# Hybrid encoder layer on one core: order of the down projection's splits, one head norm's precedence, the place of small products, and the end of the last tile but one

## The chip, the cores and the metric

The kernel runs on one core of a Trainium2 chip. The metric is the device time of one execution in microseconds (us). The core has a matrix engine (TensorE, PE), a vector engine (VectorE, DVE), a scalar engine (ScalarE, ACT), a general engine (GpSimd, POOL) and a sync engine (SyncE, SP) that here only issues DMAs; ScalarE and GpSimd issue some DMAs too. Each engine works through its own list of instructions in order; semaphores tie the lists together.

## The reference

One layer on an input x of 1024 rows of 1024 float32 numbers:

```python
h = rmsnorm(x, norm_mix_pre)
y = mixer(h, w_in, ...)            # short conv and gated linear attention, then @ w_out
x = x + rmsnorm(y, norm_mix_post)
h = rmsnorm(x, norm_ffn_pre)
y = conv_mlp(h, w_up, conv_ffn, w_down)
x = x + rmsnorm(y, norm_ffn_post)
```

The mixer projects h with w_in, runs a gated 3-tap convolution over 512 channels, and gated linear attention (GLA) forwards and backwards in chunks of 64 rows for 4 heads (key width 64, value width 128). Each head's output o is normalised over its 128 channels, `o * rsqrt(mean(o*o) + eps) * gla_head_norm`, and gated with silu. The feed-forward part (FFN) is `(silu(conv3(h W_up)_gate) * conv3(h W_up)_val) @ W_down` with an inner width of 2816.

## The kernel before

**Precision.** Each float32 operand of a large product is split into a high part in a reduced format and a low rest: `split` (L690) makes the high part as a cast on ScalarE (L691) and the low part as a subtraction on VectorE (L692). Each product takes three passes (high with high, high with low, low with high).

**Stages**, by their place in the trace: first norm and value projection 0 to 66 us, gates 66 to 111, GLA and convolution 111 to 325, output projection 325 to 440, FFN up in 22 columns 440 to 841, FFN down 841 to 1055, the last norm and the stores to 1063. A tile framework sets the order of each engine's list: it issues instructions by the program's order and by precedence, and buffers of a pool are handed on as they come free.

**GLA.** `feature_chunk` (L230) computes 128 columns of a projection, in 8 parts of 6 matmuls of 512 columns. After each part it takes one entry off a list `between` and issues it. `gla_head` (L478) appends three entries (L590): the eight products `kv` for the first half of the chunks, the eight for the second, and the 32 score products (sc). They need `koT`, a copy by ScalarE (L524). After each kv, ScalarE copies it into the states S (L565, L569), and VectorE runs the recurrence over them (L574, L578). A head's output `po` is then squared by ScalarE into `on`, and its norm follows (L614 to L616): a reduction on VectorE, the reciprocal square root in `rstd_of` (one-column steps: L175 and L177 on ScalarE, L176 and L181 to L184 on VectorE), and the product `on`. TensorE then transposes `on` (L622, into pot).

**FFN down.** A Strassen-like scheme replaces 8 block products by 7, numbered m. `big_product` (L1117) runs m = 2, 1, 3, 6, 5, 7, each over q = 0 to 10 with 12 matmuls of 512 columns. `operands(m, q)` (L1080) prepares one q: a raw tile from a small pool is filled by SyncE with a block of the activations (L1087) and one of the weights or of their sums (L1090 or its neighbour), and then split. Below, d2_4 stands for m = 2, q = 4; the profile cuts such names to d_4, d_4r (raw), d_4h and d_4l. For q = 10 of m = 1 and 2 the activation is still in SBUF. While this starts, the last FFN column is still worked on: its convolution (L965 to L967), its silu (L1045), its gate (L1048) and the sums that the scheme needs (L1060 to L1064), which ScalarE's queue stores (L1057, L1065, L1066). GpSimd computes sums of weight blocks (L128 to L131) and loads and stores their tiles.

**The end.** The seventh product (m = 4) is done by rows, output tile by output tile. For tiles 4 to 7 ScalarE squares the parts (L1203), VectorE multiplies by the gain (L1207) and adds parts (L1202), `rstd_of` follows, and `finish` (L1171) computes yg times the row's factor plus x2, the residual, in one VectorE instruction (L1174), and stores it. The last tile (t = 7) is worked in parts of 256 columns and finished in two halves.

Of the kernel before, what the change touches and what calls it, by code (L numbers as in the profile page):

```python
# [8 lines left out]
F32 = mybir.dt.float32  # L9
F32R = mybir.dt.float32r  # L10
I32 = mybir.dt.int32
AF = mybir.ActivationFunctionType
# [4 lines left out]
P = 128  # L17
# [3 lines left out]
NT = L // P  # L21
HALF = 512
HEADS = 4
DK = 64
DV = 128
# [4 lines left out]
NFC = FF // P  # L30
# [11 lines left out]
def kernel(  # L42
# [20 lines left out]
    nc = tc.nc  # L63
    x = x[0]
    out = out[0]
# [16 lines left out]
    def ps_tile(name):  # L82
        return psp.tile([P, 1024], F32, tag="ps", name=name)

    def act_tile(name):
        return actp.tile([P, KT, HALF], F32R, tag="act", name=name)
# [77 lines left out]
    def keep(ins):  # L164

        return tc.keep_in_program_order(ins) if pinned[0] else ins

    def rstd_of(ss, width, rest=None):

        n = ss.shape[1]  # L170
        v = small.tile([P, n], F32, tag=f"rv{n}", name="rv")
        a = small.tile([P, n], F32, tag=f"rs{n}", name="rs")
        t = small.tile([P, n], F32, tag=f"rt{n}", name="rt")
        bias = eps[:, 0:1] if rest is None else rest
        keep(nc.scalar.activation(a, ss, AF.Ln, bias=bias, scale=1.0 / width))  # L175
        keep(nc.vector.tensor_scalar(v, ss, 1.0 / width, bias, op0=ALU.mult, op1=ALU.add))  # L176
        keep(nc.scalar.activation(a, a, AF.Exp, scale=-0.5))  # L177
        if n == 1:
            keep(nc.vector.scalar_tensor_tensor(t, a, v[:, 0:1], a, op0=ALU.mult, op1=ALU.mult))
        else:  # L180
            nc.vector.tensor_mul(t, a, a)  # L181
            nc.vector.tensor_mul(t, t, v)
        keep(nc.vector.tensor_scalar(t, t, -0.5, 1.5, op0=ALU.mult, op1=ALU.add))
        keep(nc.vector.tensor_mul(a, a, t))  # L184
        return a
# [42 lines left out]
    between = []  # L228
# [53 lines left out]
    with ExitStack() as n1:  # L282
# [45 lines left out]
        def norm_stats(t):  # L328
            hs[t] = h = np_.tile([P, D], F32, tag="h", name=f"h{t}")
            ss = small.tile([P, 1], F32, tag="ss", name=f"ss{t}")  # L330
            keep(nc.scalar.activation(h, xts[t], AF.Square, accum_out=ss))
            return rstd_of(ss, D)
# [38 lines left out]
        rs = norm_stats(0)  # L371
# [8 lines left out]
        order = [(0, 0), (1, 0), (0, 2), (1, 2), (2, 0), (3, 0), (0, 1), (1, 1), (2, 1), (3, 1), (2, 2), (3, 2)]  # L380
# [12 lines left out]
        order = [(k, i) for i in (0, 2, 1) for k in range(KT)]  # L393
# [74 lines left out]
    def unit(tag, name, dt=F32, bufs=1):  # L468
        return mp.tile([P, L], dt, tag=tag, name=name, bufs=bufs)
# [8 lines left out]
    def gla_head(h):  # L478
# [15 lines left out]
        m = unit("m", f"m{h}")  # L494
# [82 lines left out]
        def step_b(c):  # L577
            nc.vector.scalar_tensor_tensor(S[DK:P, c - 1, :], S[DK:P, c, :], dec[DK:P, c : c + 1], S[DK:P, c - 1, :],  # L578
                                           op0=ALU.mult, op1=ALU.add)

        def scan():
# [5 lines left out]
            for c in range(7, 0, -1):  # L587
                step_b(c)

        for group in (((states, 0), (states, 1)), ((states, 2), (states, 3)), [(scores, i) for i in range(4)]):  # L590
            between.append(lambda group=group: [step(i) for step, i in group])
        yield

        po = ps_tile(f"po{h}")
# [3 lines left out]
        for inner in (True, False):  # L598
            for c in range(NC) if inner else (c for g in range(0, NC, 4) for c in (g, g + 2, g + 1, g + 3)):
                t, par = divmod(c, 2)  # L600
                o0 = par * HALF + t // 2 * DV
                o = po[t % 2 * CH : (t % 2 + 1) * CH, o0 : o0 + DV]
# [8 lines left out]
        ov = on.rearrange("p (t d) -> p t d", d=DV)  # L611
        nc.scalar.activation(on, po, AF.Square)
        ss = small.tile([P, NT], F32, tag="ssh", name=f"ssh{h}")
        nc.vector.reduce_sum(out=ss, in_=ov, axis=mybir.AxisListType.X)  # L614
        rs = rstd_of(ss, DV)
        nc.vector.tensor_mul(ov, po.rearrange("p (t d) -> p t d", d=DV), rs.unsqueeze(2).to_broadcast([P, NT, DV]))  # L616
        yield

        pt = ps_tile(f"pot{h}")
# [36 lines left out]

    fill = conv_steps()
    gla = [gla_head(h) for h in range(HEADS)]
    for h in range(1, HEADS):
        swish_gate(h)  # L660
# [26 lines left out]
    def act2_tile(name, shape=(P, KT, HALF)):  # L687
        return act2.tile(list(shape), F32R, tag="act2", name=name)

    def split(hi, lo, src):  # L690
        nc.scalar.copy(hi, src)  # L691
        nc.vector.tensor_sub(lo, src, hi.bitcast(F32))  # L692

    cvp = ffn.enter_context(tc.tile_pool(name="cvp", bufs=3))
    korder = [4, 5, 6, 7, 0, 1, 2, 3]
# [9 lines left out]
    for k, home in zip(korder, homes):  # L705
        raw = rawp.tile([P, D], F32, tag="raw", name=f"wo{k}r")
        nc.sync.dma_start(out=raw, in_=w_out[k * P : (k + 1) * P, :])
        if len(home) == 1:
            both = mp.tile([P, 2, D], F32R, tag=home[0], name=f"wo{k}")
            wo[k] = both[:, 0, :], both[:, 1, :]  # L710
        else:
            wo[k] = tuple(piece(tag, f"wo{k}{c}") for tag, c in zip(home, "hl"))
        with tc.issue_after(last_act[0].ins):
            split(*wo[k], raw)
    yS = [(act_tile(f"yh{i}"), act_tile(f"yl{i}")) for i in range(2)]

    def split_y(hf):
        for k in korder:
            split(yS[hf][0][:, k, :], yS[hf][1][:, k, :], yT[k][:, hf * HALF : (hf + 1) * HALF])
# [78 lines left out]
    def w_tile(name, shape):  # L798
        n_w[0] += 1
        pool = wpool if n_w[0] % 10 < 6 else w2p  # L800
        return pool.tile(shape, F32R, tag="w", name=name)
# [15 lines left out]
    def raw_tile(shape, name, ring=2):  # L817

        n_raw[0] += 1
        if ring == 2 and n_raw[0] % 6 >= 3:  # L820
            return cvp.tile(shape, F32, tag="r", name=name)
        return rawp.tile(shape, F32, tag="raw", name=name)
# [213 lines left out]
    act_after = {}  # L1036
    last = {}
# [42 lines left out]
    def operands(m, q):  # L1080

        raw = raw_tile([P, 2, HALF], f"d{m}_{q}r")
        w = which[m]

        here = m < 3 and q == NQ - 1
        if not here:
            nc.sync.dma_start(out=raw[:, 0, :], in_=act_d[q][:, w[0], :])  # L1087
        if w[1] is None:
            r = (2 * q + w[2]) * P
            nc.sync.dma_start(out=raw[:, 1, :], in_=w_down[r : r + P, w[3] : w[3] + HALF])  # L1090
        else:
            nc.sync.dma_start(out=raw[:, 1, :], in_=wd_d[q][:, w[1], :])
        if m == 2 and q < 4:
            h, l = (w_tile(f"d{m}_{q}{x}", [P, 2, HALF]) for x in "hl")
        else:
            if q % 2 == 0:
                n_op[0] += 1
                open_tile[0] = act2_tile(f"d{m}_{q}") if n_op[0] % 7 in (1, 3, 5) else act_tile(f"d{m}_{q}")
            b = open_tile[0][:, 4 * (q % 2) : 4 * (q % 2) + 4, :]
            h, l = b[:, 0:2], b[:, 2:4]  # L1100
        with tc.issue_after(act_after[NFC - 2].ins) if m == 2 and q >= 4 else ExitStack():
            if here:
                split(h[:, 1], l[:, 1], raw[:, 1])
                split(h[:, 0], l[:, 0], last[m][:, 0:HALF])
            else:
                split(h, l, raw)
        return h, l

    open_tile = [None]

    def passes(o, h, l, t, start, stop, r=slice(0, HALF)):
        sl = slice(t * P, (t + 1) * P)
# [4 lines left out]
    def big_product(m, banks, start):  # L1117
        for q in range(NQ):
            h, l = operands(m, q)
            for t in range(4):  # L1120
                passes(banks[t], h, l, t, start and q == 0, q == NQ - 1)
# [5 lines left out]
    lo, hi = slice(0, HALF), slice(HALF, D)  # L1127
# [31 lines left out]
    nc.scalar.copy(y[4][:, lo], pb[0])  # L1159
    done_a = nc.scalar.copy(y[NT - 1][:, 256:HALF], pb[3][:, 256:HALF])  # L1160
    ops4 = [operands(4, q) for q in range(NQ)]

    def out_tile(t):
        x2 = raw_tile([P, D], f"x2r{t}")
        (nc.gpsimd if t < 4 else nc.sync).dma_start(out=x2, in_=x2d[t])  # L1165
        o = w_tile(f"o{t}", [P, D]).bitcast(F32)
        yg = w_tile(f"yg{t}", [P, D]).bitcast(F32)
        ss = small.tile([P, 3], F32, tag="ssf", name=f"ssf{t}")
        return x2, o, yg, ss

    def finish(t, x2, yg, o, rs):  # L1171

        for r in (lo, hi) if t == NT - 1 else (slice(0, D),):
            nc.vector.scalar_tensor_tensor(o[:, r], yg[:, r], rs[:, 0:1], x2[:, r], op0=ALU.mult, op1=ALU.add)  # L1174
            (nc.gpsimd if t < 4 else nc.sync).dma_start(out=out[t * P : (t + 1) * P, r], in_=o[:, r])

    for t in range(4):
        x2, o, yg, ss = out_tile(t)
        with tc.issue_after(done_a.ins), tc.issue_after(done_v.ins):
            nc.scalar.activation(o, y[t], AF.Square, accum_out=ss[:, 0:1])  # L1180
            nc.vector.tensor_mul(yg, y[t], gpost2)
            finish(t, x2, yg, o, rstd_of(ss[:, 0:1], D))
    for t in range(4):
        r4 = 4 + t
        x2, o, yg, ss = out_tile(r4)
# [6 lines left out]
        for i, (e0, e1) in enumerate(zip(edges, edges[1:])):  # L1192
# [6 lines left out]
            src = bank[:, r]  # L1199
            if fresh:  # L1200
                src = y[r4][:, r]
# [38 lines left out]
```

## Time and profile before

| | us |
|---|---|
| median of 3 runs | 1064.96 |
| lowest and highest | 1064.24, 1067.04 |
| the profiled execution | 1065.09 |
| its span | 1063.1 |
| TensorE busy | 1045.8 (98%) |
| VectorE busy | 800.1 (75%) |
| ScalarE busy | 466.3 (44%) |
| GpSimd busy | 344.0 (32%) |

The span is the time from the first to the last instruction of the profiled execution; its own time is 2.0 longer. Rows of a timeline have a start, a duration, the engine, the line of the kernel, the operation, what is written and read, the shapes, a count, and in brackets the engine's idle time before the row and what ended it. The view of waits lists what an engine waited for: total us, times, longest. Matmuls are pipelined: one of 512 columns shows as 0.39 us, though the next starts 0.227 us after it.

### The profile page before, as it was taken

Reading aid. Unit: us, or ns where it says so; the run is one execution under the profiler, and the core shown is the slowest. Engines: PE = TensorE matmul, PEld = TensorE weight load, DVE = VectorE, ACT = ScalarE, POOL = GpSimd, SP = SyncE. Lnnn points to the kernel's source line nnn. Section 1 sums busy time; section 2 is a strip of 40 time slices with the busy share of each in tenths; the row PEclk is TensorE's granted clock in tenths of the full one; section 3 lists DMA queues with packets and bytes.
Section 4 is the critical chain, followed back from the end, with each engine's and each line's share of the span. In section 5 each row is a group of like instructions: output and inputs, shape, how many; then the busy total and the mean of one; then the engine's idle time right before and its main releaser. Section 6 shows DMA issues by size and latency. Waiting matters only on the chain.

```text
span 1063.1 us, 14378 instructions
## 1 busy us (share of the span) xinstructions
PE 1045.8 (98%) x5409; PEld 871.3 (82%) x5409; DVE 800.1 (75%) x992; ACT 466.3 (44%) x654; POOL 344.0 (32%) x360
## 2 busy tenths in 40 slices
PE   8999999999999999999999999999999999999996
PEld 8998887788888888888888888888888777888886
DVE  6951369879868457999988988888898967556567
ACT  6431354553435334644444444444443534254452
POOL 2789500000000000004565564655656447400000
PEclk9999999999999999999999999999999999999999
DMA  8887511110156222167777876866886788976755
GB/s 286 278 274 256 182 41 33 47 41 21 45 174 187 81 80 79 50 192 249 257 250 254 283 258 229 263 201 210 278 274 229 275 326 292 359 235 220 241 177 218
DMA packets 163511, 210.64 MB, mean 198 GB/s; under 512 B 18273, under 2 KB 113650, under 8 KB 163442
## 3 DMA queue, kind: packets, MB, share of 16 engines
q1 hardware_dynamic: 142578, 134.48, 39.7%
q0 software_dynamic: 20288, 73.41, 19.6%
q10 hardware_dynamic: 576, 1.84, 0.5%
q8 instruction: 42, 0.69, 0.3%
q14 instruction: 27, 0.22, 0.1%
HBM read 146.52 MB, written 63.18 MB: 197 GB/s over the span
## 4 chain that ended last, share of the span: by engine, by line
PE 68%; DVE 14%; DMA 10%; ACT 4%; issue 4%; SPq 1%; DVEq 0%; ACTq 0%
PE pb L808 16%; PE pc L808 11%; PE pa L808 9%; PE pw L738 8%; PE pgc L238 4%; PE pgo L238 4%; DVE d L692 4%; PE pv L349 4%; PE pgv L238 3%; PE pqk L238 3%; PE pgb L238 2%; DMA d_3r<-in_w_down_dram 1%; ACT d L691 1%; DMA d_7r<-wdd 1%; DMA d_9r<-in_w_down_dram 1%
## 5 line engine op out<-in xcount | busy, mean ns | idle before, releaser
L103 POOL COPY wu10g<-pace 128x1 f32<-128x1 f32 x1 | 0.4, 355 | 362.7 <-ACT pace L995 362.7
L1114 PE MATMUL pdb<-d 128*128 128x512 f32 (+1 forms) x495 | 109.8, 383 | 1.2 <-DVE d L692 1.2
L1114 PEld LDWEIGHTS pdb<-d 128*128 128x128 f32 x495 | 90.7, 188 | 20.0 <-DVE d L692 2.0
L808 PE MATMUL pb<-t,uv 128*128 128x512 f32 x264 | 63.5, 389 | 0.0
L808 PEld LDWEIGHTS pb<-t,uv 128*128 128x128 f32 x264 | 49.6, 188 | 10.3
L992 DVE TENSOR_TENSOR cg<-cv,pb 128x512 f32<-128x512 f32 x22 | 15.1, 685 | 33.6 <-issue 19.0
L1045 ACT ACTIVATE uu<-uu 128x1024 f32<-128x1024 f32 x22 | 23.4, 1062 | 37.4 <-DVE uu L967 37.4
L1165 POOL DMA_DIRECT2D x2r<-x2d x4 | 2.1, 535 | 110.0 <-DMA d_8r<-actd 100.3
L1048 DVE TENSOR_TENSOR uu<-uu,uv 128x1024 f32<-128x1024 f32 x22 | 34.0, 1546 | 0.0
L966 DVE SCALAR_TENSOR_TENSOR uu<-cg,prm,uu 128x1023 f32<-128x1023 f32 x22 | 29.1, 1323 | 1.9
L1114 PE MATMUL pdc<-d 128*128 128x512 f32 x132 | 30.1, 389 | 0.0
L1114 PE MATMUL pdd<-d 128*128 128x512 f32 x132 | 30.1, 389 | 0.0
L967 DVE SCALAR_TENSOR_TENSOR uv<-cv,prm,uv 128x1023 f32<-128x1023 f32 x22 | 29.1, 1323 | 0.0
L967 DVE SCALAR_TENSOR_TENSOR uu<-cg,prm,uu 128x1023 f32<-128x1023 f32 x22 | 29.0, 1319 | 0.0
L966 DVE SCALAR_TENSOR_TENSOR uv<-cv,prm,uv 128x1023 f32<-128x1023 f32 x22 | 29.0, 1318 | 0.0
L1114 PEld LDWEIGHTS pdc<-d 128*128 128x128 f32 x132 | 24.8, 188 | 5.2
L1114 PEld LDWEIGHTS pdd<-d 128*128 128x128 f32 x132 | 24.8, 188 | 5.1
L877 ACT COPY cv<-pa 128x512 f32<-128x512 f32 x22 | 12.8, 589 | 36.5 <-PE pa L808 34.6
L965 ACT ACTIVATE uv<-cv,prm 128x1024 f32<-128x1024 f32 x22 | 25.4, 1154 | 5.2 <-DVE cv L1025 4.2
L574 DVE SCALAR_TENSOR_TENSOR S<-S,dec 64x128 f32<-64x128 f32 x56 | 19.2, 344 | 10.7 <-ACT S L565 8.5
L965 ACT ACTIVATE uu<-cg,prm 128x1024 f32<-128x1024 f32 x22 | 25.3, 1149 | 0.3 <-ACT d L691 0.3
L578 DVE SCALAR_TENSOR_TENSOR S<-S,dec 64x128 f32<-64x128 f32 x56 | 19.7, 352 | 1.9
(1314 smaller groups left out, 3237.9 us busy)
## 6 DMA issues: line engine op xcount, KB each, us to landing
actd<-as SPq DMA_DIRECT2D x20, 512.0 KB
x<-in_x_dram SPq DMA_DIRECT2D x16, 512.0 KB, 6.0
actd<-uu SPq DMA_DIRECT2D x10, 512.0 KB, 3.9
x2d<-x SPq DMA_DIRECT2D x8, 512.0 KB, 3.2
actd<-uu SPq DMA_DIRECT2D x10, 256.0 KB, 3.8
x2r<-x2d POOLq DMA_DIRECT2D x4, 512.0 KB, 5.7
x2r<-x2d SPq DMA_DIRECT2D x4, 512.0 KB, 4.2
out_dram<-o POOLq DMA_DIRECT2D x4, 512.0 KB, 6.2
```

The costliest lines, as they stand in the source:

```text
L238: nc.tensor.matmul(o[hf], wt[:, k, :], act[hf][a][:, k, :], start=(k == 0 and wt is wh and a == 0), stop=(k == KT - 1 and wt is wl))
L349: keep(nc.tensor.matmul(ps[:, n * 512 : n * 512 + VH], a[:, k, sl], w[:, k % 2, n * VH : (n + 1) * VH], start=(j == 0), stop=(j == 3 * KT ...
L578: nc.vector.scalar_tensor_tensor(S[DK:P, c - 1, :], S[DK:P, c, :], dec[DK:P, c : c + 1], S[DK:P, c - 1, :], op0=ALU.mult, op1=ALU.add)
L692: nc.vector.tensor_sub(lo, src, hi.bitcast(F32))
L738: ins = nc.tensor.matmul(ps[:, n * HALF : (n + 1) * HALF], a[:, k, sl], w[:, n * HALF : (n + 1) * HALF], start=(i == 0 and q == 0), stop=( ...
L808: nc.tensor.matmul(o, w[:, k, :], m[:, k, :], start=start and k == 0 and q == 0, stop=k == 3 and q == 2, skip_group_check=True)
L965: nc.scalar.activation(u, src, AF.Copy, scale=ffn_tap(1, r))
L966: nc.vector.scalar_tensor_tensor(u[:, 1:L], src[:, 0 : L - 1], ffn_tap(0, r), u[:, 1:L], op0=ALU.mult, op1=ALU.add)
L967: nc.vector.scalar_tensor_tensor(u[:, 0 : L - 1], src[:, 1:L], ffn_tap(2, r), u[:, 0 : L - 1], op0=ALU.mult, op1=ALU.add)
L1045: last_act[0] = nc.scalar.activation(ug, ug, AF.Silu)
L1048: nc.vector.tensor_mul(ug, ug, uv)
L1114: nc.tensor.matmul(o, a[:, 0, sl], b[:, 1, r], start=start and i == 0, stop=stop and i == 2, skip_group_check=True)
```

## The change

There are four edits.

1. `split` returns its two instructions, and `operands` keeps those of the last split in `so_far`. Each split of the down projection is issued after both instructions of the one before it, in the order of use. (For q = 10 of m = 1 and 2 there are two splits; the first is not kept.)
2. Head 0's norm, from the reduction to the product `on`, is issued with high priority.
3. An empty entry goes to the head of each head's `between` list, so that kv and scores come one part of `feature_chunk` later.
4. For tile 6 `finish` has ScalarE multiply yg by the row's factor, GpSimd add x2 and GpSimd issue the store. Before, it was one VectorE instruction and a store by SyncE.

```diff
@@ -587,6 +587,7 @@
             for c in range(7, 0, -1):
                 step_b(c)
 
+        between.append(lambda: None)
         for group in (((states, 0), (states, 1)), ((states, 2), (states, 3)), [(scores, i) for i in range(4)]):
             between.append(lambda group=group: [step(i) for step, i in group])
         yield
@@ -611,9 +612,11 @@
         ov = on.rearrange("p (t d) -> p t d", d=DV)
         nc.scalar.activation(on, po, AF.Square)
         ss = small.tile([P, NT], F32, tag="ssh", name=f"ssh{h}")
-        nc.vector.reduce_sum(out=ss, in_=ov, axis=mybir.AxisListType.X)
-        rs = rstd_of(ss, DV)
-        nc.vector.tensor_mul(ov, po.rearrange("p (t d) -> p t d", d=DV), rs.unsqueeze(2).to_broadcast([P, NT, DV]))
+
+        with tc.high_priority() if h == 0 else ExitStack():
+            nc.vector.reduce_sum(out=ss, in_=ov, axis=mybir.AxisListType.X)
+            rs = rstd_of(ss, DV)
+            nc.vector.tensor_mul(ov, po.rearrange("p (t d) -> p t d", d=DV), rs.unsqueeze(2).to_broadcast([P, NT, DV]))
         yield
 
         pt = ps_tile(f"pot{h}")
@@ -688,8 +691,7 @@
         return act2.tile(list(shape), F32R, tag="act2", name=name)
 
     def split(hi, lo, src):
-        nc.scalar.copy(hi, src)
-        nc.vector.tensor_sub(lo, src, hi.bitcast(F32))
+        return nc.scalar.copy(hi, src), nc.vector.tensor_sub(lo, src, hi.bitcast(F32))
 
     cvp = ffn.enter_context(tc.tile_pool(name="cvp", bufs=3))
     korder = [4, 5, 6, 7, 0, 1, 2, 3]
@@ -1098,15 +1100,20 @@
                 open_tile[0] = act2_tile(f"d{m}_{q}") if n_op[0] % 7 in (1, 3, 5) else act_tile(f"d{m}_{q}")
             b = open_tile[0][:, 4 * (q % 2) : 4 * (q % 2) + 4, :]
             h, l = b[:, 0:2], b[:, 2:4]
-        with tc.issue_after(act_after[NFC - 2].ins) if m == 2 and q >= 4 else ExitStack():
+        with ExitStack() as order:
+
+            for ins in so_far:
+                order.enter_context(tc.issue_after(ins.ins))
+            if m == 2 and q >= 4:
+                order.enter_context(tc.issue_after(act_after[NFC - 2].ins))
             if here:
                 split(h[:, 1], l[:, 1], raw[:, 1])
-                split(h[:, 0], l[:, 0], last[m][:, 0:HALF])
+                so_far[:] = split(h[:, 0], l[:, 0], last[m][:, 0:HALF])
             else:
-                split(h, l, raw)
+                so_far[:] = split(h, l, raw)
         return h, l
 
-    open_tile = [None]
+    open_tile, so_far = [None], []
 
     def passes(o, h, l, t, start, stop, r=slice(0, HALF)):
         sl = slice(t * P, (t + 1) * P)
@@ -1170,6 +1177,12 @@
 
     def finish(t, x2, yg, o, rs):
 
+        if t == NT - 2:
+
+            nc.scalar.activation(o, yg, AF.Copy, scale=rs[:, 0:1])
+            nc.gpsimd.tensor_add(o, o, x2)
+            nc.gpsimd.dma_start(out=out[t * P : (t + 1) * P, :], in_=o)
+            return
         for r in (lo, hi) if t == NT - 1 else (slice(0, D),):
             nc.vector.scalar_tensor_tensor(o[:, r], yg[:, r], rs[:, 0:1], x2[:, r], op0=ALU.mult, op1=ALU.add)
             (nc.gpsimd if t < 4 else nc.sync).dma_start(out=out[t * P : (t + 1) * P, r], in_=o[:, r])
```

How the lists move. TensorE in head 1's feature chunk, before (pgc is the chunk's product, kv and sc the small products; x2 are two alike):

```order
L238 MATMUL pgc_1808<-hTh_108,gc1h 128x512
L557 MATMUL kv_0_1815<-V_115,koT_1799 128x128 x2
L557 MATMUL kv_0_1815<-V_116,koT_1799 128x128 x2
L557 MATMUL kv_0_1815<-V_117,koT_1799 128x128 x2
L557 MATMUL kv_0_1815<-V_118,koT_1799 128x128 x2
L238 MATMUL pgc_1808<-hTh_110,gc1h 128x512
```

and now:

```order
L238 MATMUL pgc_1808<-hTh_108,gc1h 128x512
L238 MATMUL pgc_1808<-hTh_110,gc1h 128x512
L238 MATMUL pgc_1808<-hTl_109,gc1h 128x512
L238 MATMUL pgc_1808<-hTl_111,gc1h 128x512
L238 MATMUL pgc_1808<-hTh_108,gc1l 128x512
L238 MATMUL pgc_1808<-hTh_110,gc1l 128x512
L557 MATMUL kv_0_1821<-V_115,koT_1799 128x128 x2
L557 MATMUL kv_0_1821<-V_116,koT_1799 128x128 x2
```

The first kv comes five large matmuls later. In heads 1 to 3 seven stood ahead of kv_0, then five and six; now twelve, six and six stand ahead of kv_0, kv_1 and the scores. In head 0 it was eleven, one and six.

VectorE at head 0's norm, before and now in one piece (gv1l is the split of a later weight, ssh the norm's sum):

```order
 L517 TENSOR_TENSOR cum_1592<-cum_1592,kd_1421 128x1024
+L617 TENSOR_REDUCE ssh_1705<-on_1703 128x8
 L197 TENSOR_TENSOR gv1l<-gv1r,gv1h 128x1024
-L614 TENSOR_REDUCE ssh_1705<-on_1703 128x8
 L176 TENSOR_SCALAR rv<-ssh_1705,eps 128x8
```

The reduction moves ahead of one split; the rest keeps its place.

VectorE at the start of the down projection, before (d_1r to d_10r are the raw tiles of m = 2; L966, L967 and L1048 belong to the last FFN column):

```order
L692 TENSOR_TENSOR d_4_7229<-d_4r,d_4_7229 128x1024
L692 TENSOR_TENSOR d_4_7229<-d_5r,d_4_7229 128x1024
L1025 TENSOR_TENSOR cv_6968<-cv_6968,pb_6982 128x512
L692 TENSOR_TENSOR d_1l<-d_1r,d_1h 128x1024
L692 TENSOR_TENSOR d_6_7264<-d_6r,d_6_7264 128x1024
L1022 TENSOR_TENSOR cg_6995<-cg_6995,pc_7046 128x512
L966 SCALAR_TENSOR_TENSOR uv_7088<-cv_6968,prm,uv_7088 128x1023
L692 TENSOR_TENSOR d_2l<-d_2r,d_2h 128x1024
L967 SCALAR_TENSOR_TENSOR uv_7088<-cv_6968,prm,uv_7088 128x1023
L966 SCALAR_TENSOR_TENSOR uu_7092<-cg_6995,prm,uu_7092 128x1023
L692 TENSOR_TENSOR d_3l<-d_3r,d_3h 128x1024
```

and now:

```order
L1027 TENSOR_TENSOR cv_6968<-cv_6968,pb_6982 128x512
L694 TENSOR_TENSOR d_1l<-d_1r,d_1h 128x1024
L968 SCALAR_TENSOR_TENSOR uv_7088<-cv_6968,prm,uv_7088 128x1023
L1024 TENSOR_TENSOR cg_6995<-cg_6995,pc_7046 128x512
L969 SCALAR_TENSOR_TENSOR uv_7088<-cv_6968,prm,uv_7088 128x1023
L694 TENSOR_TENSOR d_2l<-d_2r,d_2h 128x1024
L968 SCALAR_TENSOR_TENSOR uu_7092<-cg_6995,prm,uu_7092 128x1023
L694 TENSOR_TENSOR d_3l<-d_3r,d_3h 128x1024
L969 SCALAR_TENSOR_TENSOR uu_7092<-cg_6995,prm,uu_7092 128x1023
L694 TENSOR_TENSOR d_4_7229<-d_4r,d_4_7229 128x1024
L694 TENSOR_TENSOR d_4_7229<-d_5r,d_4_7229 128x1024
```

The splits of q = 4 and 5 stand behind that of q = 3, and q = 6 comes behind L1050, the gate of the last column. SyncE's loads are reissued in the order in which the splits free the raw tiles: d2_9's load, for instance, moves behind the first two of m = 1, and follows d2_7's split.

ScalarE's last rows, before (tile 6 is ssf_8599, the last tile ssf_8653):

```order
L175 ACTIVATE rs<-ssf_8599 128x1
L177 ACTIVATE rs<-rs 128x1
L1203 ACTIVATE o_8651,ssf_8653<-pdb_7355 128x256
L1203 ACTIVATE o_8651,ssf_8653<-y_7147 128x256
L175 ACTIVATE rs<-ssf_8653 128x1
```

and now:

```order
L175 ACTIVATE rs<-ssf_8599 128x1
L177 ACTIVATE rs<-rs 128x1
L1182 ACTIVATE o_8597<-yg_8598,rs 128x1024
L1216 ACTIVATE o_8652,ssf_8654<-pdb_7355 128x256
L1216 ACTIVATE o_8652,ssf_8654<-y_7147 128x256
L175 ACTIVATE rs<-ssf_8654 128x1
```

The copy for tile 6 stands ahead of both squares of the last tile. On VectorE the instruction L1174 of tile 6 is gone and nothing else moves; GpSimd's list ends with the addition and the store of tile 6, which left SyncE's list.

## The prediction

> **What bounds the kernel now.** I read the page first, then busy time by stretch, then TensorE's waits, and then the timeline around each wait. The page's head and engine rows:
>
> ```profile
> span 1063.1 us, 14378 instructions
> PE 1045.8 (98%) x5409; PEld 871.3 (82%) x5409; DVE 800.1 (75%) x992; ACT 466.3 (44%) x654; POOL 344.0 (32%) x360
> ```
>
> Busy time by stretch, for FFN up, down and the end (columns: stretch, its length, each engine's busy time and instructions, granted clock, DMA share, GB/s):
>
> ```profile
> 440.00:841.00 401.00, 400.43 (x1764) 330.28 (x1763) 354.00 (x353) 175.57 (x214) 203.29 (x199) 1.00 0.73 239
> 841.00:1055.00 214.00, 211.10 (x958) 174.78 (x956) 139.00 (x155) 94.54 (x130) 50.37 (x53) 1.00 0.77 265
> 1055.00:1063.10 8.10, 0.05 (x1) 0.00 (x0) 3.94 (x11) 1.01 (x4) 0.00 (x0) 0.74 0.33 130
> ```
>
> TensorE bounds the kernel: it has work 98% of the span, at full clock, and one 512-wide matmul goes out every 0.227 us (401.00 / 1764). No edit removes a matmul. So the change can win only the small gaps in which TensorE waits, and the 8.1 us after its last matmul. The gaps (line waited for, total us, times, longest):
>
> ```profile
> PE pot L622 <- DVE on L616: 1.8, 1, 1.8
> PE pdb L1114 <- DVE d L692: 1.2, 1, 1.2
> PE pda L1114 <- DVE d_2l L692: 1.0, 1, 1.0
> PE pda L1114 <- DVE d_3l L692: 0.7, 1, 0.7
> PE kv L557 <- ACT koT L524: 0.6, 2, 0.3
> ```
>
> These five rows, 5.3 us by the view, are all that the first three edits can aim at. Counted from start to start of the matmuls a wait costs 0.1 to 0.2 more, since the pipeline restarts: d_2l below is 847.79 - 846.45 - 0.227 = 1.11 where the view says 1.0.
>
> **Head 0's norm.** VectorE, ScalarE and TensorE around that wait:
>
> ```profile
> 182.25 1.22 DVE L197 TENSOR_TENSOR gv1l<-gv1r,gv1h 128x1024 fp32r<-128x1024 f32 x1
> 183.38 1.22 DVE L614 TENSOR_REDUCE ssh<-on 128x8 f32<-128x1024 f32 x1
> 184.63 0.30 ACT L175 ACTIVATE rs<-ssh,eps 128x8 f32<-128x8 f32 x1 [3.69 <-DVE ssh L614]
> 185.21 0.17 DVE L181 TENSOR_TENSOR rt<-rs 128x8 f32<-128x8 f32 x1 [0.34 <-ACT rs L177]
> 187.46 1.07 PE L622 MATMUL pot<-ident,on 128*128 128x128 f32 x8 [1.76 <-DVE on L616]
> ```
>
> The order puts the reduction one row ahead of gv1l's split and nothing else. The norm then starts 1.13 us earlier (183.38 - 182.25), but gv1l's split still runs inside it: it ends at 182.25 + 1.13 + 1.14 = 184.5, while ScalarE's two steps end before that. So L181 goes from 185.21 to about 184.65, and pot wins 0.56, not 1.13 and not the 1.8 of the wait. gv1l itself is 1.1 late for no one: TensorE is one feature chunk away from it. **-0.56.**
>
> **Small products one part on.** On TensorE each head's kv_0 moves behind five more matmuls of 0.227 in heads 1 to 3 (+1.135) and one in head 0; kv_1 and the scores move by six. The kv row holds two waits of 0.3, one in head 0 and one in head 2 (0.4 each with the restart). Head 2's goes. In head 0 one matmul covers 0.23 of it, and this is lost again where TensorE, earlier by it, waits for `on`. What is late next is the chain behind kv, in head 1:
>
> ```profile
> 191.13 1.01 ACT L487 COPY kd<-pqk 64x1024 f32<-64x1024 f32 x1 [0.69 <-DVE kd L486]
> 192.17 0.58 ACT L565 COPY S<-kv 64x512 f32<-64x512 f32 x1
> 193.86 2.24 DVE L574 SCALAR_TENSOR_TENSOR S<-S,dec 64x128 f32<-64x128 f32 x6 [2.76 <-ACT S L565]
> 193.86:229.06 35.20, 35.20 (x274) 28.86 (x271) 32.80 (x53) 14.69 (x19) 0.00 (x0) 1.00 0.11 31
> 227.83 1.23 DVE L616 TENSOR_TENSOR on<-po,rs 128x1024 f32<-128x1024 f32 x1
> 229.53 0.71 PE L622 MATMUL pot<-ident,on 128*128 128x128 f32 x5
> ```
>
> Here kv_0 was done at about 192.1 and its copy was held by the kd copy that ends at 192.14. Five matmuls later, less the 0.56 won, kv_0 ends at 192.67: S and VectorE's scan start 0.5 later. From 193.86 to 229.06 VectorE is busy for 32.80 of 35.20, so most of that arrives at head 1's norm. Its pot had only 229.53 - 229.06 = 0.47 in hand, 0.32 beyond the 0.15 that passed from `on` to pot in head 0 (186.08 + 1.23 to 187.46, where 186.08 is the multiplication's start; the wait itself shows that it was last). So head 1's pot waits 0.5 + 0.56 - 0.32 = 0.74, and after it TensorE stands 0.18 later than before. Then head 2 gives 0.4. Stage 111 to 325: **-0.2**; between +0.8 (the scan late by the whole 1.135 in head 1, 0.32 of it covered) and -1.2 (0.56, 0.4 and 0.23 in full).
>
> **Down projection, splits in order of use.** VectorE at the start of the stage, and TensorE's first wait:
>
> ```profile
> 838.01 1.71 DVE L692 TENSOR_TENSOR d<-d_4r,d 128x1024 fp32r<-128x1024 f32 x1
> 839.63 2.31 DVE L692 TENSOR_TENSOR d<-d_5r,d 128x1024 fp32r<-128x1024 f32 x1
> 846.45 0.39 PE L1114 MATMUL pda<-d_2h 128*128 128x512 f32 x1
> 846.52 1.22 DVE L692 TENSOR_TENSOR d_2l<-d_2r,d_2h 128x1024 fp32r<-128x1024 f32 x1
> 847.79 0.50 PE L1114 MATMUL pda<-d_2l,d_2h 128*128 128x512 f32 x1 [0.96 <-DVE d_2l L692]
> ```
>
> The splits of q = 4, 5 and 6, needed only at 854 and later, stood ahead of 2 and 3. They now stand behind both: 1.71 + 2.31 + 1.21 less on VectorE ahead of d_2l, whose split starts at about 844 and is needed at 846.7. Both starting waits go (1.1 and, with the restart, 0.9), and so does the wait on pdb (1.4 with the restart), which is d1_4's: its split had stood behind those of d1_5 and d1_6. That is 3.4 at most. Behind this lie the loads, because a raw tile is refilled only after its split. Three loads, d2_9, d1_2 and d1_9 (the trace cuts d2_9 to d_9r), and the split of d1_10:
>
> ```profile
> 856.88 0.43 SPq L1090 DMA_DIRECT2D d_9r<-in_w_down_dram  x1
> 861.00 1.05 ACT L691 CAST d<-d_9r 128x1024 fp32r<-128x1024 f32 x1 [3.88 <-DVE uu L1048]
> 864.01 0.57 SPq L1090 DMA_DIRECT2D d_2r<-in_w_down_dram  x1
> 874.80 1.06 ACT L691 CAST d<-d_2r 128x1024 fp32r<-128x1024 f32 x1 [6.39 <-DMA d_2r<-in_w_down_dram]
> 894.31 1.05 ACT L691 CAST d<-d_9r 128x1024 fp32r<-128x1024 f32 x1 [7.11 <-DMA d_9r<-in_w_down_dram]
> 900.20 1.93 DVE L692 TENSOR_TENSOR d<-d_10r,d 128x512 fp32r<-128x512 f32 x1
> 901.71 0.98 PE L1114 MATMUL pdb<-d 128*128 128x512 f32 x3
> ```
>
> d1_10's split ends at 902.13, and the second of its matmuls (901.71 + 2 x 0.227) starts at 902.16: it is just in time now, with TensorE 3.4 late. To keep all of the gain it must come 3.4 earlier; its load follows d1_8's split, which the tie now puts behind d1_4's. The whole chain of splits and loads starts earlier too, since VectorE reaches the last column's sums sooner and ScalarE stores them sooner; I take four fifths of the 3.4 as kept, and give 0.7 back here (an estimate, between 0 and 3.4). d2_9's load is issued at about 858, behind d2_7's split and the sums ahead of that. TensorE wants its first matmul at 846.45 + 7 x 12 x 0.227 = 865.5 and its low half at 865.7; less cast and subtraction (1.05 + 1.22) the load must be down by 863.4. Before it took 4.1 at most (856.88 to the cast at 861.00, which waited for VectorE); d1_2's took 10.8 (864.01 to 874.80). I take 5.8, near the first, since it is its own row: 0.4 of wait. **-3.4 + 0.7 + 0.4 = -2.3**.
>
> **Last tile but one.** First, what GpSimd does beside VectorE, and ScalarE's price:
>
> ```profile
> 839.15 1.71 POOL L131 TENSOR_TENSOR wd11r<-wd11r 128x512 f32<-128x512 f32 x1
> 853.91 1.29 POOL L129 TENSOR_TENSOR wd12r<-wd13r,wd12r 128x512 f32<-128x512 f32 x1
> L965 ACT ACTIVATE uv<-cv,prm 128x1024 f32<-128x1024 f32 x22 | 25.4, 1154 | 5.2 <-DVE cv L1025 4.2 <-DVE as L1063 1.1
> ```
>
> Then the tail:
>
> ```profile
> 1051.30 0.37 ACT L1203 ACTIVATE o<-pdb 128x256 f32<-128x256 f32 x1
> 1054.29 1.28 DVE L1174 SCALAR_TENSOR_TENSOR o<-yg,rs,x2r 128x1024 f32<-128x1024 f32 x1
> 1055.95 0.41 DVE L1202 TENSOR_TENSOR y<-y,pdl 128x256 f32<-128x256 f32 x1
> 1058.13 1.41 DVE L1174 SCALAR_TENSOR_TENSOR o<-yg,rs,x2r 128x512 f32<-128x512 f32 x2
> ```
>
> VectorE loses 1.28 us at 1054.29, and TensorE ends at 1055.05, so y<-y,pdl could start 0.9 earlier. It does not: in ScalarE's order the copy (1.15, 1054.3 to 1055.45) now stands ahead of the last tile's first square, which ran at 1051.30. That square ends at 1055.85, its sum is read, and VectorE's ssf step ahead of y<-y,pdl waits for it. y<-y,pdl: 1055.95 before, 1056.0 to 1056.2 now. Then GpSimd's add of 128x1024 runs from 1055.5 for 2 x 1.29 = 2.6 at most (an estimate from the 512-wide row; I take 2.4), to about 1057.9. Beside such an add d_5's split took 2.31 instead of 1.22: it waited until the add's end at 840.86 and then ran. yg<-y,gpost, two SBUF operands, follows y<-y,pdl in VectorE's queue, and would so wait from 1056.4 to 1057.9; it would end at 1058.3, the four one-column steps behind it (0.17 each in L181's row, some 0.2 with the way between them) at 1059.1, where the last pair started at 1058.13, and the last store follows. GpSimd's own store is out before that. **+1.0**; 0 if nothing blocks, 2.1 if the ssf step waits as well (y<-y,pdl then starts at 1058.1).
>
> The Trainium skill has this as a rule (SBUF — State Buffer, "Who interferes with whom"): one of the two engines gets the shared port pair for the whole instruction, and a VectorE instruction with two SBUF inputs contends with a GpSimd one that reads SBUF. The rows at 839 agree. By the same section `tensor_scalar` can enter a mode that uses both pairs, which would make it the 2.1 case; no row of before shows a VectorE step of one column beside a GpSimd add.
>
> **Sum**, against the profiled execution (1065.09; its span 1063.1 and 2.0 around it): -0.2 - 2.3 + 1.0 = -1.5, 1063.6. It stands 0.13 above the median, 1064.96; so 1063.5. About 0.3%, 3.2 us, is what a measurement of this kernel can tell from no change.
>
> **Rivals.** (a) Everything aimed at is won and nothing is late behind it: -3.4 and -1.2, tail 0: 1064.96 - 4.6 = 1060.4. For it: the waits are short and most later splits stand well ahead of their use; against: the just-in-time d1_10, and two-operand VectorE work beside the add. 0.25. (b) The down gain is wholly returned at d1_9 and d1_10, since loads and not the order set them (ScalarE waited 7.11 us for d_9r): -0.2 + 0 + 1.0, 1065.8. 0.13. (c) Slower: d2_9's load falls into the crowd. Issued at 858 with the 10.8 us of d1_2's it lands at 868.8, its split ends at 871.1, TensorE wants it at 865.7: 5.4 of wait. With -3.4, -0.2 and +1.0 that is +2.8: 1067.8. It turns the sign from a landing at 866.0 on (2.6 of wait). Against it: it is issued 6 us ahead of d1_2's. 0.12, half of it above 1068.2, with a further wait at d1_10.
>
> My forecast has 0.50, 1062.2 to 1064.9. The range of 8 in 10 takes in most of (a), all of (b) and the start of (c): 1060.0 to 1066.8. Faster by over 0.3% (below 1061.8): most of (a) and a little of the forecast's lower edge, 0.27. Slower (above 1068.2): 0.08. Within: 0.65.
>
> **What would show it.** Right: no waits for d_2l, d_3l and d1_4, but one of 0.3 to 1.5 at d2_9, d1_9 or d1_10; head 0's pot wait at 1.2 to 1.4 and a new one at head 1's of about 0.7; a last VectorE pair that starts 3.0 to 4.5 us after TensorE's end (3.1 before), with a yg<-y,gpost of about 1.9 us. Wrong: a last pair that starts earlier than 3.1 after TensorE's end; no new wait in the down projection, or one over 2 us; head 1's pot without a wait.

## The result, and the profile after

| | before | changed |
|---|---|---|
| median of 20 runs | 1065.38 | 1072.33 |
| lowest and highest | 1063.15, 1069.06 | 1064.18, 1077.62 |
| ratio to before, 95% interval (not the quotient of the medians, which is 1.0065) | | 1.0051 [1.0033, 1.0069] |
| profiled execution, its span | 1065.09, 1063.1 | 1077.45, 1075.7 |

The change makes the kernel slower by about half a per cent, and it scatters: before, 20 executions lie within 6 us; changed, within 13.4. The profile shows a long execution; of three later profiles of the same kernel two show a long one and one a short one. From the first profile's waits of TensorE:

```profile
PE pda L1121 <- ACT d L694: 8.6, 1, 8.6
PE pdb L1121 <- DVE d L694: 2.2, 2, 2.1
PE pot L625 <- DVE on L619: 1.5, 1, 1.5
PE pda L1121 <- DVE d L694: 1.4, 2, 1.0
PE pb L810 <- DVE cv L1016: 1.2, 2, 0.8
PE pot L625 <- ACT gv2h L196: 0.6, 1, 0.6
```

The waits on d_2l and d_3l are gone. In their place stands one of 8.6 us, for a cast of the same product, m = 2. (The last row belongs to head 1's pot; what ended it is told under the small products below.) By the starts of TensorE's first matmuls, the stages are (us, between the marks named):

| stage | before | changed | difference |
|---|---|---|---|
| first qk product to head 0's pot | 76.59 | 76.09 | -0.50 |
| to head 1's pot | 42.08 | 42.89 | +0.81 |
| to head 2's pot | 42.44 | 42.09 | -0.35 |
| to head 3's pot | 41.63 | 41.54 | -0.09 |
| FFN up | 423.30 | 424.93 | +1.63 |
| down, m = 2 | 32.21 | 42.95 | +10.74 |
| down, m = 1 | 31.66 | 32.75 | +1.09 |
| last matmul to the span's end | 8.05 | 6.91 | -1.14 |

A product of 11 x 12 matmuls without a wait takes 29.92 (m = 3 and later runs below show it). So the loss is in one place: of the 13.0 us that m = 2 takes beyond this, the wait for d2_9 is 8.8, counted from start to start, and 1.0 more follows for its low half; 1.1 is a wait for d2_7's low half, which VectorE reaches late, and most of the rest is a slower clock behind the long wait, told below. The chain that ended last names the place (start, duration, what): the split of d2_7, SyncE's issue, the load, the cast behind it:

```profile
862.58 1.15 DVE d L694
863.73 0.02 SPq L1089
863.75 0.03 issue
863.78 0.33 SPq L1089
864.11 0.05 issue
864.16 12.59 DMA d_9r<-in_w_down_dram
876.75 0.02 issue
876.77 0.02 ACTq L694
876.79 0.04 issue
876.83 1.05 ACT d L694
```

d2_9's load goes out at 863.8, where before it went at 856.5 to 856.9, and takes 12.6 us instead of at most 4.1. The raw tile came free only with d2_7's split. VectorE ahead of that split:

```profile
851.76 1.22 DVE L694 TENSOR_TENSOR d<-d_4r,d 128x1024 fp32r<-128x1024 f32 x1
852.90 2.32 DVE L694 TENSOR_TENSOR d<-d_5r,d 128x1024 fp32r<-128x1024 f32 x1
855.14 2.31 DVE L1050 TENSOR_TENSOR uu<-uu,uv 128x1024 f32<-128x1024 f32 x1
857.38 2.31 DVE L694 TENSOR_TENSOR d<-d_6r,d 128x1024 fp32r<-128x1024 f32 x1
859.61 1.77 DVE L1062 TENSOR_TENSOR as<-uu,uu 128x512 f32<-128x512 f32 x1
...
862.50 1.21 DVE L694 TENSOR_TENSOR d<-d_7r,d 128x1024 fp32r<-128x1024 f32 x1
```

and GpSimd in the same time:

```profile
851.87 2.27 POOL L128 TENSOR_TENSOR wd12r<-wd12r 128x512 f32<-128x512 f32 x1 [3.25 <-DMA wd12r<-in_w_down_dram]
854.22 2.16 POOL L129 TENSOR_TENSOR wd12r<-wd13r,wd12r 128x512 f32<-128x512 f32 x1
856.45 2.15 POOL L130 TENSOR_TENSOR wd13r<-wd13r,wd12r 128x512 f32<-128x512 f32 x1
...
859.13 1.70 POOL L131 TENSOR_TENSOR wd13r<-wd13r 128x512 f32<-128x512 f32 x1
...
861.89 0.53 POOL L123 DMA_DIRECT2D wd19r<-in_w_down_dram  x1
```

The two engines take turns: each step of VectorE takes 2.31 instead of 1.22 (1.77 instead of 0.68), and three of GpSimd's four sums take 2.15 to 2.27, the last 1.70, instead of 1.29. d2_7's split ends 3 x 1.1 + 1.1 = 4.4 later than it would alone. By then GpSimd has finished its sums and issues three loads of 512 KB (from 861.89 on), ScalarE stores the last column's sums, and d2_9's load stands among them.

### The profile page after: what moved, and what is told of

It reads as the page before. It is cut to its first block, busy times and chain, and to the rows that moved or that the text cites. A ratio compares the mean times of both kernels' runs of the same rounds, so it can differ in the third digit from the quotient of the medians.

```text
span 1075.7 us, 14393 instructions
## 1 busy us (share of the span) xinstructions
PE 1047.6 (97%) x5409; PEld 871.2 (81%) x5409; DVE 801.0 (74%) x991; ACT 467.1 (43%) x655; POOL 348.4 (32%) x362
## 4 chain that ended last, share of the span: by engine, by line
PE 80%; DVE 10%; DMA 5%; issue 3%; ACT 2%; SPq 0%; DVEq 0%; ACTq 0%
PE pb L810 15%; PE pc L810 10%; PE pa L810 8%; PE pw L740 8%; PE pdb L1121 8%; PE pgc L238 4%; PE pgo L238 4%; PE pv L349 4%; PE pgv L238 3%; PE pqk L238 3%; PE pdd L1121 3%; PE pdc L1121 3%; PE pgb L238 2%; DVE d L694 2%; DMA d_9r<-in_w_down_dram 1%
## 5 line engine op out<-in xcount | busy, mean ns | idle before, releaser
L1050 DVE TENSOR_TENSOR uu<-uu,uv 128x1024 f32<-128x1024 f32 x22 | 32.4, 1474 | 0.0
L1121 PE MATMUL pda<-d 128*128 128x512 f32 x84 | 22.0, 418 | 10.2 <-ACT d L694 8.6
L969 DVE SCALAR_TENSOR_TENSOR uv<-cv,prm,uv 128x1023 f32<-128x1023 f32 x22 | 30.7, 1394 | 0.0
L968 DVE SCALAR_TENSOR_TENSOR uv<-cv,prm,uv 128x1023 f32<-128x1023 f32 x22 | 30.1, 1368 | 0.0
L574 DVE SCALAR_TENSOR_TENSOR S<-S,dec 64x128 f32<-64x128 f32 x56 | 19.2, 344 | 14.0 <-ACT S L565 11.7
L1121 PEld LDWEIGHTS pda<-d 128*128 128x128 f32 x84 | 16.6, 201 | 15.5 <-ACT d L694 9.1
L967 ACT ACTIVATE uv<-cv,prm 128x1024 f32<-128x1024 f32 x22 | 25.4, 1155 | 5.8 <-DVE cv L1027 5.2
```

Of the source, the lines that this page charges most:

```text
L574: nc.vector.scalar_tensor_tensor(S[0:DK, c + 1, :], S[0:DK, c, :], dec[0:DK, c : c + 1], S[0:DK, c + 1, :], op0=ALU.mult, op1=ALU.add)
L967: nc.scalar.activation(u, src, AF.Copy, scale=ffn_tap(1, r))
L968: nc.vector.scalar_tensor_tensor(u[:, 1:L], src[:, 0 : L - 1], ffn_tap(0, r), u[:, 1:L], op0=ALU.mult, op1=ALU.add)
L969: nc.vector.scalar_tensor_tensor(u[:, 0 : L - 1], src[:, 1:L], ffn_tap(2, r), u[:, 0 : L - 1], op0=ALU.mult, op1=ALU.add)
L1050: nc.vector.tensor_mul(ug, ug, uv)
L1121: nc.tensor.matmul(o, a[:, 0, sl], b[:, 1, r], start=start and i == 0, stop=stop and i == 2, skip_group_check=True)
```

## The experiments

Theory 1 is this: the tie puts d2_9's load behind a split that VectorE reaches late, and so into a crowd of transfers. Theory 2: the loss comes from the other three edits. Theory 3: the tied order makes VectorE late, whatever the loads do. Each median below stands beside one of the kernel before that was measured with it.

**The tie alone** (tie_only): the kernel before with `so_far` and the new `split`, nothing else.

> The kernel before with the tie of the splits alone. Theory 1 (a load in the crowd: the tie puts d2_9's load behind a late split of d2_7, among ScalarE's stores and GpSimd's loads): slower than before by 4 to 9 us, and scattered over some 10 us from execution to execution, as the changed kernel is; a wait of several us at d2_9 in the profile. Theory 2 (the loss comes from the other three edits, the tie only closes gaps): 1 to 3 us faster than before, scattered no more than before.

Measured: 1073.53 (1072.62 to 1074.37) against 1065.78, ratio 1.0075 [1.0057, 1.0092]. d2_9's load goes out at 861.93, its cast runs at 873.25, TensorE waits 7.2. Theory 2 falls. The scatter that was expected did not show: six executions lie within 1.8 us.

**Without the tie** (no_tie): the changed kernel with the old lines in `operands`.

```diff
...
-            for ins in so_far:
-                order.enter_context(tc.issue_after(ins.ins))
...
```

> The changed kernel without the tie: norm precedence, small products one part on, the end by ScalarE and GpSimd. Theory 1: no loss, 0 to 1.5 us faster than before, scattered as before. Theory 2: 4 to 9 us slower than before.

Measured: 1066.69 (1065.56 to 1068.45) against 1065.78, ratio 1.0010 [1.0000, 1.0020]: no loss of the size of theory 2, but not the gain of 0 to 1.5 that theory 1 gave it either. The waits on d_2l and d_3l are back (1.0 and 0.8).

**The changed kernel with five raw tiles in turn** (tie_ring5). The pool of three that the raw tiles share holds `gpost2` for good at this stage, so it has two left, while the rotation asks it for three in a row: d2_7, d2_8, d2_9 on two buffers. Here two are asked of it, then three of the other:

```diff
-        raw = raw_tile([P, 2, HALF], f"d{m}_{q}r")
+        n_raw[0] += 1
+        n_ring[0] += 1
+        pool, tag = (rawp, "raw") if n_ring[0] % 5 in (2, 3) else (cvp, "r")
+        raw = pool.tile([P, 2, HALF], F32, tag=tag, name=f"d{m}_{q}r")
```

> The changed kernel, with the raw tiles of the down projection taken in turn from five buffers, so that each load waits for the split five back, and d2_9's for that of d2_4 instead of d2_7. Theory 1: d2_9's load goes out at about 853 and is down before the crowd; the wait of 8.8 us goes, and with it the scatter; 1060 to 1062. Theory 3 (the tied order itself makes VectorE late, whatever the loads do): still over 1067.

Measured: 1062.92 (1060.10 to 1069.32) against 1065.78, ratio 0.9973 [0.9957, 0.9989]. The tied order stands, and the loss is gone: d2_9's load goes out at 851.7, and its cast, at 856.55, waits for no DMA:

```profile
851.74 0.42 SPq L1095 DMA_DIRECT2D d_9r<-in_w_down_dram  x1
```

VectorE is no earlier: it reaches d2_7's split at 861.16. The longest wait of the down projection is now 0.9, and it is for that split; this much is what VectorE's lateness costs where no load hangs on it. Theory 3 falls as the cause of the loss. The median is 0.9 above the range given, and the scatter did not go: ten executions lie within 4.5 us, and one stands at 1069.32.

**Five raw tiles, without the change** (ring5_only): the same diff on the kernel before.

> The kernel before with the five raw tiles in turn and no edit of the change. Theory 1: the waits on d_2l and d_3l (1.1 and 0.9) stay, since they are a matter of VectorE's order, and only the wait at d1_4 (1.4) can go: 0 to 1.5 us faster than before. Theory 3 says the same, 0 to 1.5 faster. If the tie is not needed once loads are early, 2 to 3.4 us faster.

Measured: 1061.65 (1061.10 to 1066.08), ratio 0.9968 [0.9951, 0.9985]: 4.1 faster than before, where 0 to 1.5 was expected of it, or 2 to 3.4 if the tie was not needed. With loads that go out earlier, the scheduler's own order of splits also comes out better (the two causes were not tried apart): of the waits at the start only d_3l's stays (0.5), and m = 2 and m = 1 take 30.81 and 29.92.

**The tie with five raw tiles, without the other edits** (tie_ring).

> The kernel before with the tie and the five raw tiles in turn, without the other three edits. Theory 1: no wait over 1 us in the down projection: 1060 to 1062, 0.5 to 1.5 faster than the changed kernel with five raw tiles. Set against five raw tiles alone (1061.65) it shows what the tie is worth once loads are early: at most the 0.7 of d_3l's wait, less what the tie costs at the last FFN column.

Measured: 1060.87 (1059.67 to 1063.15) against 1066.00, ratio 0.9954 [0.9938, 0.9970]. This is the fastest version here, faster than before and than the change, and 2.0 under the changed kernel with five raw tiles, where 0.5 to 1.5 was expected. Its interval overlaps that of five raw tiles alone, so the tie's own worth, 0.8 by the medians, is not settled.

**GpSimd's sums taken away** (memsets): the changed kernel, which here leaves out the four sums of the weight pair q = 6 and writes zeros into the same tiles instead.

```diff
+        if q == 6:
+            for w in (w1, w1, w1, w1, w2, w2, w2, w2):
+                nc.gpsimd.memset(w, 0.0)
+        else:
...
```

> The changed kernel, where GpSimd's four sums of one weight pair (q = 6), which run beside VectorE's work at 850 to 862, are eight memsets that only write and take about as long; the sums of that pair are left out. If d2_7's split is late because VectorE's two-operand steps wait for GpSimd's sums (2.31 instead of 1.22 four times over): these steps take 1.2, the split of d2_7 ends some 4 us earlier, d2_9's load is issued at 858 to 860 ahead of GpSimd's loads, and the median is 1063 to 1068. If the order alone makes it late: the load stays at 862 to 864 and the median at 1071 to 1074.

Measured: 1066.06 (1063.43 to 1068.04) against 1066.00, ratio 0.9994 [0.9978, 1.0011]: 6 us less than the changed kernel. VectorE, SyncE and GpSimd:

```profile
851.51 1.21 DVE L1054 TENSOR_TENSOR uu<-uu,uv 128x1024 f32<-128x1024 f32 x1
852.65 1.21 DVE L698 TENSOR_TENSOR d<-d_6r,d 128x1024 fp32r<-128x1024 f32 x1
...
855.59 1.21 DVE L698 TENSOR_TENSOR d<-d_7r,d 128x1024 fp32r<-128x1024 f32 x1
...
855.27 0.96 POOL L130 MEMSET wd12r<- 128x1024 f32 x1
...
857.24 0.91 SPq L1096 DMA_DIRECT2D d_9r<-in_w_down_dram  x1
```

Beside writes that read nothing, VectorE's steps take 1.21, d2_7's split ends at 856.8 and the load goes out at 857.2. m = 2 and m = 1 take 29.92 each: no wait at all in 264 matmuls, with the tie. (In the profile part of the gain is lost again, because m = 4 then waits for ScalarE:

```profile
PE pdb L1125 <- ACT y L1171: 1.6, 1, 1.6
```

a copy that TensorE reached later in the long executions. The same row stands at 0.8 in the short execution below.) So lateness comes from the two engines' sums, not from the order. The replacement also let the scheduler put one GpSimd sum ahead of the third of its loads, so the crowd was a little thinner too; that share isn't separated.

**Three more profiles of the changed kernel** (after_again, after_look3, after_look4).

> The changed kernel once more, for a second profile. Theory 1: the time goes with the wait at d2_9 and nothing else: at some 1065 the wait is under 2 us, at 1075 it is 8 to 10; the load of d2_9 is issued earlier, against GpSimd's three loads, in the shorter execution.

> The changed kernel, one more look, for an execution of under 1068, which some 7 of 20 were. Theory 1: in such a one the splits of d_4 to d_6 and the sums on VectorE take less of GpSimd's time or come earlier, d2_9's load goes out before 861, and the wait there is under 2 us. In an execution of over 1070 the load goes out at 862 to 864 and the wait is 6 to 9. If a short execution shows the load as late as the long ones, or the long wait somewhere else, theory 1 doesn't explain the scatter.

> As for the look before it: under 1068 the load of d2_9 goes out before 861 with a wait under 2 us; over 1070 at 862 to 864 with 6 to 9.

| execution | d2_9's load issued | its cast | m = 2 takes | time |
|---|---|---|---|---|
| first profile | 864.16 | 876.83 | 42.95 | 1077.45 |
| after_again | 862.93 | 873.74 | 42.66 | 1074.15 |
| after_look4 | 861.72 | 872.26 | 42.07 | 1073.60 |
| after_look3 | 857.00 | 864.34 | 30.53 | 1063.72 |

The wait at d2_9 was 6.8 at 1074.15 and 6.5 at 1073.60, a little under the 8 to 10 expected of the first of these, and 0.3 in the short execution, which shows what the scatter is. In it VectorE, GpSimd and SyncE go so:

```profile
850.13 1.22 DVE L694 TENSOR_TENSOR d<-d_5r,d 128x1024 fp32r<-128x1024 f32 x1
851.27 1.21 DVE L1050 TENSOR_TENSOR uu<-uu,uv 128x1024 f32<-128x1024 f32 x1
852.40 1.22 DVE L694 TENSOR_TENSOR d<-d_6r,d 128x1024 fp32r<-128x1024 f32 x1
...
855.35 1.22 DVE L694 TENSOR_TENSOR d<-d_7r,d 128x1024 fp32r<-128x1024 f32 x1
...
851.01 8.43 POOL L128 TENSOR_TENSOR wd12r<-wd12r 128x512 f32<-128x512 f32 x1 [3.21 <-DMA wd12r<-in_w_down_dram]
...
865.06 0.54 POOL L123 DMA_DIRECT2D wd19r<-in_w_down_dram  x1
...
857.00 1.32 SPq L1092 DMA_DIRECT2D d_9r<-in_w_down_dram  x1
```

GpSimd's first sum takes 8.43 us: it gets through only when VectorE's row of steps ends at 858.3. Here VectorE never gives way, so d2_9's load is early and GpSimd's loads late (865.06, not 861.89). In the long executions the two alternate, and GpSimd's loads go out ahead of d2_9's. It is the same program with the same lists, and 10 us lie between them. Even here the load took up to 7.3 us (857.00 to the cast at 864.34), beside two stores of ScalarE's (issued at 855.46 and 857.19) and ahead of all of GpSimd's three loads. So those loads alone do not make the crowd, and what each transfer adds to it was not tried apart.

**Small products alone** (c_only): `between.append(lambda: None)` on the kernel before.

> The kernel before with the small products one part on, alone. In the instruction lists this edit alone moves head 0's reduction ahead of the split of gv1l; the precedence alone moves nothing. So pqk to head 0's pot should be 0.5 us shorter and head 0's pot to head 1's 0.8 longer here too; with the last 0.3 to 0.5 of head 2 that is 0.1 won in GLA, and if the wait of 1.0 to 1.6 us at column 17 of FFN up comes with this edit, 0.3 to 1.0 us slower than before in all. If that wait comes from elsewhere: 0.1 faster.

Measured: 1065.91 (1062.41 to 1070.55) against 1066.00, ratio 0.9999 [0.9982, 1.0017]. The time tells nothing apart; the trace does: 76.10, 42.89, 42.09 and 41.54 between the marks of the table above, as in the changed kernel to 0.01. So both the half microsecond at head 0's pot and the new wait at head 1's come with this edit alone. In the instruction lists it is this edit that moves the reduction of head 0's norm ahead of gv1l's split; with the precedence alone no engine's list differs from before (that kernel was not run). FFN up took 422.87 here, without the wait at column 17 that the expectation asks about; that wait is also missing from the three later profiles of the changed kernel, so it does not come with every execution, and one profile doesn't show what it comes with.

**The last tile but one alone** (d_only): the new branch in `finish` on the kernel before.

> The kernel before with the end of the last tile but one by ScalarE and GpSimd, alone. If GpSimd's add holds up yg<-y,gpost in VectorE's list, as in the changed kernel without the tie (1.41 instead of 0.43): the last pair starts 3.3 to 4.1 us after TensorE's end instead of 3.1, and the median is 0.2 to 1.0 above before. If tile 6's rows come early enough that the add is over by then: pair at 2.2 to 2.4 after TensorE's end, 0 to 0.8 faster than a kernel before whose pair starts at 3.1, and no different from one whose pair starts at 2.2.

Measured: 1064.68 (1062.78 to 1067.09) against 1065.43, ratio 0.9991 [0.9974, 1.0009]: no difference. The last pair of VectorE instructions (L1174) starts 2.23 after TensorE's end, the second case, with yg<-y,gpost at 0.57. The first case did occur: without the tie GpSimd and VectorE stand so,

```profile
1057.41 2.34 POOL L1178 TENSOR_TENSOR o<-o,x2r 128x1024 f32<-128x1024 f32 x1 [9.73 <-ACT o L1177]
1058.06 0.20 DVE L1213 TENSOR_SCALAR ssf<-ssf 128x1 f32<-128x1 f32 x1
1058.18 0.41 DVE L1210 TENSOR_TENSOR y<-y,pdl 128x256 f32<-128x256 f32 x1
1058.62 1.41 DVE L1215 TENSOR_TENSOR yg<-y,gpost 128x256 f32<-128x256 f32 x1
```

and in the changed kernel's first profile so:

```profile
1066.73 2.38 POOL L1183 TENSOR_TENSOR o<-o,x2r 128x1024 f32<-128x1024 f32 x1 [10.19 <-ACT o L1182]
1068.84 0.42 DVE L1215 TENSOR_TENSOR y<-y,pdl 128x256 f32<-128x256 f32 x1 [1.24 <-PE pdl L1121]
1069.29 0.42 DVE L1220 TENSOR_TENSOR yg<-y,gpost 128x256 f32<-128x256 f32 x1
```

In the first, the step waits for the end of the add (1059.75). In the second, tile 6 is so early that the add is over (1069.11) before the step comes. With this end the last pair starts 2.2 after TensorE's end where there is no meeting (the changed kernel's first two profiles, five raw tiles, this edit alone), and 3.45, 3.54, 3.87 and 4.25 where there is (no_tie, memsets, after_look3, after_look4). Without it: 3.1 before, and 2.2 to 2.4 in the other four.

## Why the prediction was wrong

The forecast was 1063.5 and "same"; the median is 1072.33, above the range. Step by step:

- **Bound and gaps: right, with one thing left out.** No matmul went or came, and what moved is in TensorE's waits. But the forecast keeps full clock throughout, and behind the long wait it was not granted: in the first profile the granted clock is 0.5 for 10.24 us from 871.77 on, and the matmuls go out every 0.427 us instead of 0.227 until it is over. This adds about 1.1 us there, and 2.7 and 2.2 in after_again and after_look4, where the wait ends sooner and more matmuls fall into that time. So m = 2 takes 42.1 to 43.0 in all three, though the waits are 8.6, 6.8 and 6.5. In the short execution and with the memsets the clock is full in this stage.
- **Head 0's norm: size right, edit wrong.** -0.56 was forecast, -0.50 measured. But it was put down to the precedence, which alone moves no instruction. It comes with the empty entry in `between`.
- **Small products: right.** A new wait of 0.74 at head 1's pot and 0.4 back in head 2 were forecast; the marks show +0.81, -0.35 and -0.09. GLA as a whole: -0.2 forecast, -0.13 measured. The mechanism is the one forecast, though the view of waits names ScalarE's cast of gv2h: head 1's pot starts at 230.26, 0.14 after the end of its `on` (228.89 + 1.23), and before the change it started while that cast was still running (229.53, the cast from 229.28 to 230.33).
- **Down projection: the gain right, the load wrong.** The waits on d_2l, d_3l and, where the loads come in time, d1_4 do go: 29.92 and 29.92 with the memsets, against 32.21 and 31.66, make 4.0 where 3.4 was forecast. The step that failed is "d2_9's load is issued at about 858 ... I take 5.8": it was issued at 864 and took 12.6. Its mechanism stood there as rival (c), with a chance of 0.12 and a wait of 5.4; the wait was 6.5 to 8.6 in three of four profiles, by the view of waits. But (c), too, kept the issue at 858. What was left out is VectorE's time ahead of d2_7's split. The prediction gives no sum for its 858, but steps of 1.22 lead to it: 863.8, less the 4.4 of taking turns and the 1.9 by which the down projection began later (842.91 against 840.99), is 857.5. The prediction itself quotes 2.31 for d_5's split beside a GpSimd sum, and uses that row for the tail. Four steps at the higher price carry the issue from 858 to 862, and past GpSimd's loads; the later start does the rest. "It is issued 6 us ahead of d1_2's" then fails too: the two are issued 2.3 us apart.
- **d1_10: wrong.** The 0.7 to be given back there did not come in the short execution (m = 1 takes 29.92). In the first profile the late load pushed d1_4's instead (2.1 by the view).
- **Last tile but one: mechanism right, size by chance.** The blocked step is there, at 1.40 to 1.41, and the ssf step is not blocked (0.20), as the +1.0 assumed and against the 2.1. But whether the two meet depends on how early tile 6 is. ScalarE's work for that tile waits for a store to leave a buffer, and this wait ended 8.3 us before TensorE's end in the profile before (1046.79), 10.1 in the first one after (1058.70) and 11.7 with five raw tiles alone (1040.53); the forecast took the one execution as the rule. Alone (d_only) the edit is worth nothing that can be measured.
- **FFN up: not in the sum.** It varies between 422.35 and 424.93 over thirteen profiles, with waits at different columns. With the same program it was 422.61, 423.73, 423.85 and 424.93, so this is scatter of the same size as the gains forecast. In the profile with the tie alone 1.2 of it, by the view of waits, is a wait at the last column, for an add (L1010) that stands behind VectorE steps of 1.79 and 2.31 beside GpSimd's sums; whether the tie has a part in that was not tried.

The Trainium skill's rule (SBUF — State Buffer, "Who interferes with whom") was cited for the tail and should have been applied to the whole stage: the runs agree that two-operand VectorE steps and GpSimd sums exclude each other (2.31 and 2.15), and that a GpSimd instruction which only writes does not contend (1.21 beside the memsets).

Still open: what decides whether VectorE keeps the way to itself (8.43 for GpSimd) or the two alternate. One short execution was profiled. In it GpSimd's first sum began 0.88 after a VectorE step had (851.01 and 850.13), in the three long ones 0.04 to 0.11 after one (851.87 and 851.76 in the first profile); whether this decides it was not tried.

## What to carry to other kernels

When splits or other steps are put in order of use, look at what each of them releases: a load that waits for a late buffer can cost more than the gaps that the order closes, and the cheaper cure may be a rotation that uses all buffers (here 4 us, without the tie). Price a chain of VectorE steps with the engine that runs beside it, not with the duration of a step alone. Where a gain depends on two engines not meeting, one profile doesn't show how often they meet.

## What the runs showed of the hardware

- Two-operand VectorE steps and GpSimd sums ran either in turn (2.31 and 2.15 to 2.27 each, instead of 1.22 and 1.29) or with one GpSimd sum held while eight VectorE steps ran (8.43).
- A load of 512 KB in two parts took at most 4.1 us at 857 and 12.6 at 864 in the same queue, while three loads of GpSimd's and two stores of ScalarE's were under way; in the short execution it took up to 7.3 at 857, beside ScalarE's stores but before GpSimd's loads.
- VectorE's steps with one operand in PSUM (0.41) or of one column (0.20) were not held by the GpSimd add beside them.
- After TensorE had waited 6.5 to 8.6 us for d2_9 (the first profile, after_again, after_look4, tie_only), the granted clock was 0.5 for one stretch of 10.24 us, which began during the wait, and matmuls went out every 0.427 us instead of 0.227 until it ended.
